# A norm's sum in four groups, a first stage in native matmuls, the next job's weights ahead of constants and gates, splits shared by two engines, an output sum moved first

## The chip, the cores and the metric

The kernel runs on one core of one Trainium2 chip, in one launch. The metric is the device time in microseconds of one execution; three runs are given, and their median stands for the kernel. A profiled execution has a time of its own, and a span (first to last recorded instruction) that is a little shorter. Engines are named as in the profile: PE (TensorE matmul), PEld (its weight load), DVE (VectorE), ACT (ScalarE), POOL (GpSimd), SP (SyncE, which here only issues DMAs).

## The reference, cut to what matters

One decoder layer with D = 2048, 256 tokens, batch 1, float32:

```python
cond = silu(c)
sh1, sc1, g1, sh2, sc2, g2 = split(cond @ mod_w + mod_b, 6)     # 6 vectors of 2048
h = rms_norm(x, norm1_g) * (1 + sc1) + sh1
a, gt = split(h @ w_in + b_in, 2)                               # 2048 x 4096
u = depthwise_causal_conv(a * sigmoid(gt), dw_w) + dw_b         # 31 taps
y = silu(layer_norm(u, ln_g, ln_b)) @ w_out + b_out             # 2048 x 2048
x = x + (1 + g1) * y
h = rms_norm(x, norm2_g) * (1 + sc2) + sh2
x = x + (1 + g2) * (square(relu(h @ mlp_w1)) @ mlp_w2)          # 2048 x 8192 x 2048
```

The six modulation vectors cost a 2048 x 12288 matrix for one row, so they are mostly traffic: 100 MB of the 301 MB that are read.

## The kernel before, in words

The text below gives the names and lines of the kernel before. Activations are kept transposed, channels on the 128 partitions in 16 tiles (`KT`), the 256 tokens along the free axis. `k` counts channel tiles, `k2` pairs of them.

**Precision.** A float32 product is made in one of two ways. *Native*: one float32 matmul with 256 columns, which the profile records as two passes (32 records for 16 matmuls). *Split*: weight and activation are each split into a rounded `hi` (ScalarE copy to fp32r) and a remainder `lo` (`lo = w - hi`, on VectorE or GpSimd), and three fast fp32r products are summed. `split_w` (L191) splits a 1 MB weight tile in two halves of 8 channel tiles: hi at L200, lo at L202. `split_act` (L208) does it for an activation pair: hi at L209, lo at L210, into a tile `hl`.

**Loads.** All large loads are 1 MB, issued by SP in one fixed list, `order` (L460 to L472). `take` (L182) hands out the next one and `top_up` issues further loads as buffers come free: `RAW` = 5 raw tiles (one more may be issued and wait on SP's queue) and `FIRST` = 4 tiles of the first stage. SP works in order, so a load that waits for its buffer holds all behind it.

**Modulation.** Two ways again. `mod_col` (L353) takes one column tile `mod_c` and multiplies and sums it against `cond` on VectorE (L358, 2.3 us). `mod_chunk` (L291) takes a row tile `mod_r` and does it with small matmuls on TensorE (L300); these lie between the jobs as filler.

**First stage** (L490 to L594, the first 141 us). Squares of x on ScalarE, their sum over the channels by matmuls with a matrix of ones into one PSUM tile (`column_sum`, L376), then `rms_factor` (L394) and `inverse_root` (L382) give r1. After that come sixteen steps of k. A step takes two modulation columns (scale and shift of channel tile k, `take_col`, VectorE in the order of `in_order`), forms h (ScalarE, L585), and adds the product of h with one 1 MB tile `first` (16 blocks of 128 x 128) into eight PSUM accumulators `held[0..7]` (the outputs of the "in" jobs 0 to 7, value and gate). Steps whose k is in `NATIVE` are native (L548). The six others split the tile: hi on ScalarE (L525), lo on VectorE (L532), three products (L552 to L554). The last tile is loaded in two halves (L176). Behind the list of the first stage stand the rest of the constants (`dwq`, 256 columns, and the second part of `vec`, 1008 columns), and then the weights of job 8.

**Jobs.** `jobs` (L437) is the list of all that follows: ("in", 8..15), ("out", 0..7), and four quarters of ("up", ...) and ("down", ...). A job has two weight tiles c = 0, 1. The loop at L769 splits the next job's weights ahead of the job's matmuls. Of the "in" jobs the outputs go through `gate` (L744: Sigmoid on ScalarE, product on VectorE into a padded tile `u`), and then through the 31-tap convolution, for eight channel tiles on VectorE (L623) and for the others on TensorE, by way of ScalarE copies into a `wide` tile (`copy_wide`, L699 to L708) and a GpSimd-made diagonal. L758 to L767 are the seam of the two stages: weights of job 8 split, the eight gates of the held outputs, the second weight tile of job 8 split between gates 1 and 2.

**Layer norm and out jobs.** L838 to L888 make the layer norm: per pair a subtraction on GpSimd (L879), a product on VectorE (L880), two Silu on ScalarE (L884), and the split by `split_act`. The out jobs follow; of each the sum is scaled and biased on ScalarE (L905), added to x on VectorE (L907), squared, scaled for the MLP, and split again (L919 to L922). ("out", 1, 0) is split early, on GpSimd.

**What sets the order.** A tile scheduler with a timeline simulation fixes each engine's order at build time, from the order of the program, priorities and its own costs. `urgent()` (L124) raises the priority of what it encloses; `tc.issue_after(ins)` demands that an instruction comes behind another. An engine then works strictly in that order and waits on semaphores. Tiles are buffers of pools; a new use waits until all uses of the old tile are through. The `conv` pool of the second stage (L597: `wide`, `diag` and others) lies where the `start` pool (L88: x and the `first` tiles) was.

Of the kernel before, what the change touches and what calls it, by code (L numbers as in the profile page):

```python
# [11 lines left out]
ALU = mybir.AluOpType  # L12
# [24 lines left out]
NATIVE = (1, 3, 5, 6, 8, 9, 11, 12, 14, 15)  # L37
# [20 lines left out]
SIDE = 14  # L58
POOLED = [("out", 0), ("out", 1), ("up", 0, 1), ("up", 0, 2)]
# [4 lines left out]
def conv_block(ctx: ExitStack, tc: tile.TileContext, x, vec, dwq, c_row, mod_r, mod_c, w_first, w_in, w_out, w1, w2, out):  # L64
# [12 lines left out]
    soon = VEC["b_in"]  # L77
# [36 lines left out]
    nc.scalar.activation(cz[:, :, 3], col("c", 0, KT), AF.Silu)  # L114
    modc = const.tile([P, 6 * KT], F32, name="modc")
# [3 lines left out]
    warm = const.tile([P, 1], F32, name="warm")  # L119

    def table(func, after):
        nc.scalar.activation(warm, after, func)
# [3 lines left out]

    raw = {}
# [3 lines left out]
    state = {"used": 0}  # L131
# [27 lines left out]
    def top_up():  # L159
        while todo and waiting[home(todo[0])] < room[home(todo[0])]:  # L160
# [13 lines left out]
            with tc.issue_after(state["load"].ins) if "load" in state else ExitStack():  # L174
                if key == ("first", KT - 1):
                    nc.sync.dma_start(raw[key][:, 0:HELD], source(key)[:, 0:HELD])  # L176
                    with tc.issue_after(state["load"].ins):
                        state["load"] = nc.sync.dma_start(raw[key][:, HELD:], source(key)[:, HELD:])
                else:
                    state["load"] = nc.sync.dma_start(raw[key], source(key))  # L180
# [8 lines left out]
    HALF = KT // 2  # L189

    def split_w(key, engine):  # L191
# [4 lines left out]
        for h in range(2):  # L196
# [3 lines left out]
            nc.scalar.activation(hi, w[:, ks, :], AF.Copy)  # L200
            with tc.issue_after(state["e_end"]) if key[0] == "out" and engine is nc.vector else ExitStack():
                end = engine.tensor_tensor(lo, w[:, ks, :], hi.bitcast(F32), op=ALU.subtract)  # L202
            if engine is nc.gpsimd:
                state["pool"] = end.ins
# [3 lines left out]
    def split_act(dst, src):  # L208
        state["hi_end"] = nc.scalar.activation(dst[:, :, 0:T], src, AF.Copy).ins  # L209
# [130 lines left out]
    def mod_finish():  # L340
        while pending:
# [3 lines left out]
            with urgent():  # L345
# [4 lines left out]
                for b, at in enumerate(ats):  # L350
                    mod_bias(at, nj, p[:, 0 : nj * n].rearrange("p (j n) -> p n j", n=n)[:, b, :])
# [30 lines left out]
    def inverse_root(ms, src, scale, r, then=None):  # L382
# [4 lines left out]
        state["root_end"] = nc.scalar.activation(guess, guess, AF.Copy, scale=-0.5).ins  # L387
        if then is not None:
            table(then, guess[:, 0:1])
        nc.vector.scalar_tensor_tensor(ms, ms, EPS, q, op0=ALU.add, op1=ALU.mult)  # L390
        nc.vector.scalar_tensor_tensor(r, ms, 3.0, guess, op0=ALU.subtract, op1=ALU.mult)
        return r

    def rms_factor(total, ms, r):  # L394
        nc.vector.tensor_scalar(ms, total, 1.0 / D, None, op0=ALU.mult)
        return inverse_root(ms, total, 1.0 / D, r)
# [65 lines left out]
    order += [("vec", 0)]  # L462
    order += [jobs[HELD] + (c,) for c in range(2)]
# [27 lines left out]
    mods(by_col(0))  # L491
# [555 lines left out]
```

## Time and profile before

| | |
|---|---|
| three runs | 1114.11, 1112.88, 1110.83 us (median 1112.88) |
| profiled execution | 1112.13 us |
| its span | 1110.3 us |
| mean granted TensorE clock | 0.994 |
| first stage | ends at 140.9 us |
| "in" jobs 8 to 15 with the convolution | to about 300 us |
| layer norm and out jobs | to about 400 us |
| MLP, four quarters | to the end |
| read from memory | 301 MB |

How to read it: times are microseconds of the span of the profiled execution. The page gives the busy time of each engine and the chain of work that ended last. Other views of the trace are used in the prediction: TensorE's waits by what released them (total, count, longest); a view of the DMA traffic in 40 slices; the chain itself, row by row (start, length, what); the timeline of a stretch (start, length of the row, engine, line, operation, output and inputs, shape, count, and in brackets the wait ahead of it and its releaser); the table of stretches (for each engine busy time and count, then granted clock, DMA share and GB/s).

### The profile page before, as it was taken

Reading aid. Unit: us, or ns where it says so; the run is one execution under the profiler, and the core shown is the slowest. Engines: PE = TensorE matmul, PEld = TensorE weight load, DVE = VectorE, ACT = ScalarE, POOL = GpSimd, SP = SyncE. Lnnn points to the kernel's source line nnn. Section 1 sums busy time; section 2 is a strip of 40 time slices with the busy share of each in tenths; the row PEclk is TensorE's granted clock in tenths of the full one; section 3 lists DMA queues with packets and bytes.
Section 4 is the critical chain, followed back from the end, with each engine's and each line's share of the span. In section 5 each row is a group of like instructions: output and inputs, shape, how many; then the busy total and the mean of one; then the engine's idle time right before and its main releaser. Section 6 shows DMA issues by size and latency. Waiting matters only on the chain.

```text
span 1110.3 us, 15575 instructions
## 1 busy us (share of the span) xinstructions
PE 1087.4 (98%) x6112; PEld 900.7 (81%) x6112; DVE 766.0 (69%) x1018; ACT 522.5 (47%) x693; POOL 161.2 (15%) x103
## 2 busy tenths in 40 slices
PE   6999899999989999999999999999999999999998
PEld 4988776666689998888888888888888888888887
DVE  4988689988379977676785567644656565565553
ACT  5222295664575578444444444333444334444441
POOL 0000087467532334000000000000000000000000
PEclk8999999999999999999999999999999999999999
DMA  9999978889499977898996879757888867788641
GB/s 386 420 420 421 417 304 349 347 319 353 170 357 369 388 260 254 260 277 269 385 394 215 236 235 296 298 157 261 249 237 236 246 206 227 224 237 249 211 143 38
DMA packets 142027, 314.24 MB, mean 283 GB/s; under 512 B 87553, under 2 KB 105473, under 8 KB 106753
## 3 DMA queue, kind: packets, MB, share of 16 engines
q1 hardware_dynamic: 141808, 313.16, 81.0%
q8 instruction: 48, 0.79, 0.3%
q14 instruction: 25, 0.20, 0.0%
q10 hardware_dynamic: 146, 0.08, 0.0%
HBM read 301.15 MB, written 12.07 MB: 282 GB/s over the span
## 4 chain that ended last, share of the span: by engine, by line
PE 87%; DMA 6%; DVE 5%; issue 1%; ACT 0%; DVEq 0%
PE mm L248 20%; PE mm L247 20%; PE mm L249 20%; PE mm L224 6%; DMA raw<-mod_c 4%; DVE raw L358 3%; PE mm L225 3%; PE mm L221 3%; PE mm L220 3%; PE mm L222 3%; PE row L300 2%; PE mm L731 2%; DMA first<-w_first 2%; DVE lo L532 1%; PE mm L548 1%
## 5 line engine op out<-in xcount | busy, mean ns | idle before, releaser
L200 ACT ACTIVATE hi<-raw 128x1024 fp32r<-128x1024 f32 x320 | 336.0, 1058 | 373.6 <-PE mm L249 322.7
L202 DVE TENSOR_TENSOR lo<-raw,hi 128x1024 fp32r<-128x1024 f32 x272 | 333.5, 1234 | 175.1 <-ACT hi L200 171.7
L248 PE MATMUL mm<-lo,u 128*128 128x512 f32 x496 | 193.0, 389 | 0.0
L247 PE MATMUL mm<-hi,u 128*128 128x512 f32 x496 | 193.0, 389 | 0.0
L249 PE MATMUL mm<-hi,u 128*128 128x512 f32 x496 | 192.9, 389 | 0.0
L249 PE MATMUL mm<-hi,hl 128*128 128x512 f32 x480 | 186.7, 389 | 0.0
L248 PE MATMUL mm<-lo,hl 128*128 128x512 f32 x480 | 186.7, 389 | 0.0
L247 PE MATMUL mm<-hi,hl 128*128 128x512 f32 x480 | 186.7, 389 | 0.0
L358 DVE SCALAR_TENSOR_TENSOR raw<-raw,cond 128x2048 f32<-128x2048 f32 x64 | 147.6, 2310 | 32.4 <-DMA raw<-mod_c 28.6
L202 POOL TENSOR_TENSOR lo<-raw,hi 128x1024 fp32r<-128x1024 f32 x48 | 114.5, 2410 | 199.8 <-ACT hi L200 199.8
L249 PEld LDWEIGHTS mm<-hi,u 128*128 128x128 f32 x496 | 93.1, 188 | 19.4
L248 PEld LDWEIGHTS mm<-lo,u 128*128 128x128 f32 x496 | 93.1, 188 | 19.1
L247 PEld LDWEIGHTS mm<-hi,u 128*128 128x128 f32 x496 | 93.1, 188 | 19.0
L247 PEld LDWEIGHTS mm<-hi,hl 128*128 128x128 f32 x480 | 90.1, 188 | 18.8
L249 PEld LDWEIGHTS mm<-hi,hl 128*128 128x128 f32 x480 | 90.1, 188 | 18.7
L248 PEld LDWEIGHTS mm<-lo,hl 128*128 128x128 f32 x480 | 90.1, 188 | 18.7
L623 DVE SCALAR_TENSOR_TENSOR acc<-u,v,acc 128x256 f32<-128x256 f32 x224 | 94.7, 489 | 1.9
L220 PE MATMUL mm<-hl,hi 128*128 128x256 f32 x288 | 81.1, 286 | 3.0 <-DVE x L907 2.6
L221 PE MATMUL mm<-hl,hi 128*128 128x256 f32 x288 | 82.0, 286 | 0.2 <-DVE hl L210 0.2
L222 PE MATMUL mm<-hl,lo 128*128 128x256 f32 x288 | 81.7, 285 | 0.0
L224 PE MATMUL mm<-hl,hi 128*128 128x512 f32 x224 | 81.5, 404 | 0.0
L225 PE MATMUL mm<-hl,lo 128*128 128x256 f32 x224 | 63.5, 284 | 0.0
(184 smaller groups left out, 1269.5 us busy)
## 6 DMA issues: line engine op xcount, KB each, us to landing
raw<-w SPq DMA_DIRECT2D x128, 1024.0 KB, 5.3
raw<-mod_c SPq DMA_DIRECT2D x64, 1024.0 KB, 11.2
raw<-mod_r SPq DMA_DIRECT2D x32, 1024.0 KB, 7.6
raw<-w_in SPq DMA_DIRECT2D x16, 1024.0 KB, 7.1
raw<-w_out SPq DMA_DIRECT2D x16, 1024.0 KB, 7.6
first<-w_first SPq DMA_DIRECT2D x15, 1024.0 KB, 16.5
flat<-two SPq DMA_DIRECT2D x30, 256.0 KB, 2.7
two<-flat SPq DMA_DIRECT2D x120, 64.0 KB, 4.3
```

Source lines behind the costliest of these rows:

```text
L200: nc.scalar.activation(hi, w[:, ks, :], AF.Copy)
L202: end = engine.tensor_tensor(lo, w[:, ks, :], hi.bitcast(F32), op=ALU.subtract)
L220: nc.tensor.matmul(out_p, w, m[:, 0:T], start=begin, stop=False)
L221: nc.tensor.matmul(out_p, w, m[:, T : 2 * T], start=False, stop=False)
L222: state["mm_end"] = nc.tensor.matmul(out_p, lo[:, k % HALF, :], m[:, 0:T], start=False, stop=end)
L224: nc.tensor.matmul(p[:, c, :], hi[:, k % HALF, :], m, start=(k == 0), stop=(k == KT - 1))
L225: state["mm_end"] = nc.tensor.matmul(p[:, c, T : 2 * T], lo[:, k % HALF, :], m[:, 0:T], start=False, stop=(k == KT - 1), skip_group_check= ...
L247: nc.tensor.matmul(p, p_hi, hi, start=begin, stop=False)
L248: nc.tensor.matmul(p, p_hi, lo, start=False, stop=False)
L249: nc.tensor.matmul(p, p_lo, hi, start=False, stop=end)
L358: nc.vector.scalar_tensor_tensor(w, w, 1.0, cb, op0=ALU.mult, op1=ALU.mult, accum_out=acc)
L623: nc.vector.scalar_tensor_tensor(out, s, w, acc, op0=ALU.mult, op1=ALU.add)
```

## The change

**First stage.** The set `NATIVE` and all splits of the first stage go: every step is native (`first_mm` takes the raw tile). The squares of x are made by ScalarE for pairs 0 to 3 and by VectorE for pairs 4 to 7. Their sum goes with 32 columns of ones into four groups of 32 partitions, is copied once by ScalarE, and is folded by one further matmul, which gives 32 times the sum; `inverse_root` takes that scale into its constants, and a VectorE pass goes in both RMS norms. The ScalarE table for the root is asked for ahead, and the columns of step 0 come behind the squares in the program. The last two columns and the last weight tile (`SPLIT_LOADS`) are loaded in halves, and the products of those two columns are made by halves (`mod_col_halves`).

**Constants.** `soon` now reaches to the taps: b_in, dwb, lng, lnb and b_out come with the first vector load (96 columns more). The rest is loaded behind the first weight tile of job 8, not ahead of it.

**The seam.** The first weight tile of job 8 is split with high priority, its first half's lo on VectorE, the second on GpSimd. Gates 0 to 7 all have high priority; the second weight tile is asked for behind gate 5, with `issue_after` between gates and splits.

**Layer norm and out jobs.** `split_act` makes hi on ScalarE for even pairs and on VectorE for odd ones. The hi of ("out", 1, 1) comes after the last Silu. The modulation biases of `mod_finish` come after the last split (`lo_end`). The scaling on ScalarE and the addition to x of each out job become urgent.

The diff, cut:

```diff
-NATIVE = (1, 3, 5, 6, 8, 9, 11, 12, 14, 15)
+SPLIT_LOADS = [("col", SC1 * KT + KT - 1), ("col", SH1 * KT + KT - 1), ("first", KT - 1)]
-    soon = VEC["b_in"]
+    soon = VEC["dww"]
+    table(AF.Abs_reciprocal_sqrt, cond[:, KT - 1, 0:1])
...
-                if key == ("first", KT - 1):
...
+                if key in SPLIT_LOADS:
+                    first_half = nc.sync.dma_start(raw[key][:, 0:HALF], source(key)[:, 0:HALF])
+                    with tc.issue_after(first_half.ins):
+                        state["load"] = nc.sync.dma_start(raw[key][:, HALF:], source(key)[:, HALF:])
...
-            nc.scalar.activation(hi, w[:, ks, :], AF.Copy)
+            with tc.issue_after(state["silu"]) if key == ("out", 1, 1) else ExitStack():
+                state["w_hi"] = nc.scalar.activation(hi, w[:, ks, :], AF.Copy).ins
+            by = nc.vector if key == ("in", HELD, 0) and h == 0 else engine
...
-                end = engine.tensor_tensor(lo, w[:, ks, :], hi.bitcast(F32), op=ALU.subtract)
+                end = by.tensor_tensor(lo, w[:, ks, :], hi.bitcast(F32), op=ALU.subtract)
...
-    def split_act(dst, src):
-        state["hi_end"] = nc.scalar.activation(dst[:, :, 0:T], src, AF.Copy).ins
+    def split_act(dst, src, on_act=True):
+        if on_act:
+            state["hi_end"] = nc.scalar.activation(dst[:, :, 0:T], src, AF.Copy).ins
+        else:
+            nc.vector.tensor_copy(dst[:, :, 0:T], src)
...
-                    mod_bias(at, nj, ...)
+                    with tc.issue_after(state["lo_end"]) if "lo_end" in state else ExitStack():
+                        mod_bias(at, nj, ...)
...
+    def mod_col_halves(at):
+        w = take(("col", at))
+        which, k = divmod(at, KT)
+        accs = [modc[:, at : at + 1], other]
+        for h in range(2):
+            ks = slice(h * HALF, (h + 1) * HALF)
+            in_order(lambda: nc.vector.scalar_tensor_tensor(
+                w[:, ks, :], w[:, ks, :], 1.0, cond[:, ks, :], op0=ALU.mult, op1=ALU.mult, accum_out=accs[h]
+            ))
+        in_order(lambda: nc.vector.scalar_tensor_tensor(
+            accs[0], accs[0], other, col("modb", at), op0=ALU.add, op1=ALU.add
+        ))
...
-    def rms_factor(total, ms, r):
-        nc.vector.tensor_scalar(ms, total, 1.0 / D, None, op0=ALU.mult)
-        return inverse_root(ms, total, 1.0 / D, r)
+    def rms_factor(total, ms, r, times=1):
+        return inverse_root(ms, total, 1.0 / (times * D), r)
...
-    order += [("vec", 0)]
-    order += [jobs[HELD] + (c,) for c in range(2)]
+    order += [jobs[HELD] + (0,), ("vec", 0), jobs[HELD] + (1,)]
...
-        nc.scalar.activation(s, pair_of(xs, k2), AF.Square)
-        column_sum(p[:, 0:T], [s[:, j, :] for j in range(2)], k2 == 0, k2 == HALF - 1)
+        if k2 < HALF // 2:
+            nc.scalar.activation(s, pair_of(xs, k2), AF.Square)
+        else:
+            nc.vector.tensor_tensor(s, pair_of(xs, k2), pair_of(xs, k2), op=ALU.mult)
+        for j in range(2):
+            g = (2 * k2 + j) % 4
+            nc.tensor.matmul(p[32 * g : 32 * g + 32, 0:T], ones[:, 0:32], s[:, j, :], start=k2 < 2, stop=k2 >= HALF - 2)
+    mods(by_col(0))
+    with urgent():
+        part = two()[:, 0, :]
+        nc.scalar.activation(part, p[:, 0:T], AF.Copy)
+        p = ps.tile([P, 512], F32, name="row", bufs=1)
+        nc.tensor.matmul(p[:, 0:T], ones, part, start=True, stop=True)
+        r1 = tmp.tile([P, T], F32, name="r", bufs=1)
+        rms_factor(p[:, 0:T], p[:, T : 2 * T], r1, 32)
...
-    split_w(jobs[HELD] + (0,), nc.gpsimd)
     with urgent():
-        for i in range(2):
+        split_w(jobs[HELD] + (0,), nc.gpsimd)
+        take(("vec", 0))
+        with tc.issue_after(state["w_hi"]):
+            gate(0, held[0])
+        for i in range(1, 6):
             gate(i, held[i])
-    with tc.issue_after(state["sg"].ins):
-        split_w(jobs[HELD] + (1,), nc.gpsimd)
-    with urgent():
-        for i in range(2, HELD):
-            gate(i, held[i])
+        with tc.issue_after(state["sg"].ins):
+            split_w(jobs[HELD] + (1,), nc.gpsimd)
+        with tc.issue_after(state["w_hi"]):
+            gate(6, held[6])
+        gate(7, held[7])
...
-                    split_act(new_hl(k2), f)
+                    split_act(new_hl(k2), f, k2 % 2 == 0)
...
-            for c in range(2):
-                k = 2 * i + c
-                nc.scalar.activation(t2[:, c, :], t2[:, c, :], AF.Identity, scale=mcol(G1, k), bias=gb[:, k : k + 1])
             xp = pair_of(xs, i)
-            nc.vector.tensor_tensor(xp, t2, xp, op=ALU.add)
+            with urgent():
+                for c in range(2):
+                    k = 2 * i + c
+                    nc.scalar.activation(t2[:, c, :], t2[:, c, :], AF.Identity, scale=mcol(G1, k), bias=gb[:, k : k + 1])
+                nc.vector.tensor_tensor(xp, t2, xp, op=ALU.add)
```

In the changed kernel the native matmuls are line 550, the hi and lo of `split_w` lines 203 and 206, the output addition line 905, the `wide` copies line 700, the gates line 738.

83 lines of the change are left out of this document (24 added, 59 removed).

## The prediction

> **What bounds the kernel now.** I read the page first, then the chain that ended last, then TensorE's waits, the DMA view of the first 160 us, and the timeline at three places. From the page:
>
> ```profile
> span 1110.3 us, 15575 instructions
> PE 1087.4 (98%) x6112; PEld 900.7 (81%) x6112; DVE 766.0 (69%) x1018; ACT 522.5 (47%) x693; POOL 161.2 (15%) x103
> PE 87%; DMA 6%; DVE 5%; issue 1%; ACT 0%; DVEq 0%
> ```
>
> TensorE is the bound, and the 11% of the chain that is DMA and DVE must lie where TensorE waits for them. TensorE's waits from 141 us to the end:
>
> ```profile
> PE mm L220 <- DVE x L907: 2.6, 1, 2.6
> PE row L300 <- DMA raw<-mod_r: 0.8, 1, 0.8
> PE mm L220 <- ACT hl L209: 0.4, 1, 0.4
> PE mm L221 <- DVE hl L210: 0.2, 1, 0.2
> ```
>
> So after 141 us only 4.0 us are waited, 2.6 of them at one place (line 907). An edit behind 141 us pays there or nowhere, and a wait that it adds there is paid in full. Before 141 us the DMA view (40 slices of 4 us) and the chain say:
>
> ```profile
> GB/s 162 420 428 424 424 416 422 424 422 414 424 420 420 418 416 422 424 424 424 420 414 424 416 424 422 422 418 418 424 420 416 406 419 422 416 221 223 268 141 420
> 116.91 2.31 DVE raw L358 x2
> 121.53 2.22 DVE raw L358 x2
> 123.94 1.15 DVE lo L532
> 127.30 3.45 PE mm L548 x16
> 134.21 3.45 PE mm L548 x16
> ```
>
> The queue moves 420 GB/s without a pause to 140 us. The sixteen steps of the first stage need 3.15 MB each (two modulation columns and a weight tile), so a step can't be served faster than every 7.5 us. At its end TensorE runs behind the loads: step 13 waits for the last DVE split (line 532), so steps 14 and 15 stand back to back after it.
>
> **The change part by part.**
>
> *First stage, all steps native, last loads halved.* A native step starts at 127.14 and the next at 134.04: 6.90 us, under the 7.5 us of its loads. The six split steps lose 12 DVE and 12 ACT passes; DVE then has about 5.8 us of work a step. The rows of the end:
>
> ```profile
> 107.58 4.39 SPq L180 DMA_DIRECT2D raw<-mod_c  x2
> raw<-mod_c SPq DMA_DIRECT2D x1, 1024.0 KB, 15.1
> 127.14 3.61 PE L548 MATMUL mm<-two,first 128*128 128x256 f32 x16
> 127.79 2.28 DVE L358 SCALAR_TENSOR_TENSOR raw<-raw,cond 128x2048 f32<-128x2048 f32 x1
> 130.12 0.16 DVE L338 TENSOR_TENSOR modc<-modc,v 128x1 f32<-128x1 f32 x1
> 130.31 0.60 ACT L585 ACTIVATE two<-two,modc,amp 128x256 f32<-128x256 f32 x1 [5.23 <-DVE modc L338]
> 134.04 3.62 PE L548 MATMUL mm<-two,first 128*128 128x256 f32 x16
> ```
>
> The last column load is issued at 107.58 + 4.39 - 0.33 = 111.6 and lands 15.1 later, at 126.7; the one of step 14 lands a pitch earlier, at 119.2. In the change nothing ahead of them in the queue is larger except 48 KB of the vector, so I keep both. Step 14: 119.2 + 2.3 (product) + 0.2 + 0.7 (line 585) and some 0.2 of semaphores = 122.6, ending at 129.5. Step 15: the halves of its last column are done at 128.7 (the first from 126.3 to 127.5 behind the column before it, the second 1.2 more), + 0.2 + 0.7 = 129.7, just behind step 14. So it starts at 129.7, not 134.04, and the stage ends at 129.7 + 6.9 = 136.6 instead of 140.9: **-4.3 us**.
>
> *Norm's sum in four groups, squares on two engines, rsqrt table early.* Step 0 starts at 25.31 before; with the shorter chain I work it out at about 19. Step by step, TensorE gains 0.6 us on the loads and has caught up by step 7 from either start within 2.4 us, so this is cover for the native steps, and I count nothing more for it. If it failed, the stage would end up to 2.4 us later.
>
> *Next job's weights ahead of the constants.* The first weight tile of job 8 lands about 131.9 and is split by 136.5, as DVE now takes half of it. Job 8 can follow at 136.6. This goes with the -4.3.
>
> *What this meets: the order on ACT.* In the changed program as built, ACT's order after the first split is gates 0, 1, 2, then twelve `wide` copies (line 700), then gates 3, 4, 5, and only then the hi passes of job 8's second tile. The first `wide` copy waits for TensorE's last native matmul, since its buffer lies where x and the `first` tiles were. Before, all gates and those hi passes came ahead of the copies:
>
> ```profile
> 136.34 1.99 ACT L200 ACTIVATE hi<-raw 128x1024 fp32r<-128x1024 f32 x2
> 137.47 7.08 POOL L202 TENSOR_TENSOR lo<-raw,hi 128x1024 fp32r<-128x1024 f32 x3 [135.53 <-ACT hi L200]
> 138.24 0.83 ACT L746 ACTIVATE two<-mm,v 128x256 f32<-128x256 f32 x2
> 142.63 4.49 ACT L708 ACTIVATE wide<-u 32x284 f32<-32x284 f32 x10
> 146.60 0.40 PE L224 MATMUL mm<-hl,hi 128*128 128x512 f32 x1
> 146.83 0.28 PE L225 MATMUL mm<-hl,lo 128*128 128x256 f32 x1
> ```
>
> From the end of the stage, 136.6: 0.1, twelve copies of 0.449 = 5.4, three gates of 0.415 = 1.25, one hi pass 1.05, and then POOL's lo pass of 7.08/3 = 2.4 with two hand-overs of 0.1: 10.4 us, 147.0. Behind it stand the second half of job 8 on TensorE (in order), the hi passes of job 9, gates 6 and 7, and DVE's taps. TensorE reaches that lo at 136.6 + 5.9 = 142.5 and waits 4.5 us (2.3 for hi, one matmul, 2.2 for lo). Before it used that lo at 146.83, so from here the change is at **+0.2 us**: the stage's gain is gone. Taps start at about 143.9 against 142.54, which DVE's 3.7 us of idle time at 161 us covers; I count 0. Without that cover a job boundary could cost TensorE about 1 us.
>
> *Clock after that wait.* No row shows such a pair of pauses. The nearest is the pause at line 907:
>
> ```profile
> 329.51 0.28 PE L222 MATMUL mm<-hl,lo 128*128 128x256 f32 x1
> 332.41 0.58 PE L220 MATMUL mm<-hl,hi 128*128 128x256 f32 x1 [2.62 <-DVE x L907]
> 335.32 0.28 PE L221 MATMUL mm<-hl,hi 128*128 128x256 f32 x1
> 332.00:336.00 4.00, 3.59 (x19) 3.59 (x20) 4.00 (x7) 2.22 (x6) 1.05 (x1) 0.59 0.99 377
> 26.00:32.00 6.00, 6.00 (x32) 6.00 (x32) 5.96 (x8) 1.89 (x4) 0.00 (x0) 0.54 1.01 422
> ```
>
> Here a pause of 2.8 us (329.63 to 332.41) is followed by 13 matmuls in 2.9 us that take 0.12 each elsewhere: 1.35 lost, at a mean clock of 0.59. At the start (clock 0.54 for 6 us) about 3 us are lost. So 0 to 3, and I take the nearest row: **+1.35**.
>
> *Output sum first, splits shared.* The 2.8 us pause comes from DVE's order: the sum of out job 0 stands behind products and splits, the last of which followed an ACT pass that had waited for a load:
>
> ```profile
> 329.02 2.00 ACT L200 ACTIVATE hi<-raw 128x1024 fp32r<-128x1024 f32 x2 [2.55 <-DMA raw<-w_out]
> 330.54 1.22 DVE L202 TENSOR_TENSOR lo<-raw,hi 128x1024 fp32r<-128x1024 f32 x1
> 331.67 0.68 DVE L907 TENSOR_TENSOR x<-mm,x 128x512 f32<-128x512 f32 x1
> 319.75 0.69 DVE L210 TENSOR_TENSOR hl<-acc,hl 128x512 fp32r<-128x512 f32 x1 [1.00 <-ACT hl L209]
> raw<-mod_c SPq DMA_DIRECT2D x1, 1024.0 KB, 16.6
> 304.78 14.62 SPq L180 DMA_DIRECT2D raw<-mod_c  x2
> ```
>
> In the change four of the eight hi copies go to DVE, ACT needs 16 x 0.57 + 4 x 0.6 + 0.5 = 12 us from 303.3, and DVE's last norm split ends at about 316.6, not 320.4. Ahead of the sum there then stand two products and three splits, not three and four; the second product's load lands at 304.8 + 16.6 = 321.4. That gives 321.5 + 2.3 + three splits and hi waits (to 326.3) + 0.7 = 327.0, ahead of 329.6, when TensorE wants the buffer. So the pause and its slow matmuls go: 2.8 + 1.35 = **-4.1**. Late next is nothing near: the next weights are split 5 us ahead. The norm's own waits (0.4 + 0.2) stay, as its first pair keeps its path. The four DVE copies (0.6 each) fit in the 6 us that DVE idles there. Between 320 and 398 us DVE is full in before too, starts 3.8 us earlier and does no more, so I count 0; if the loads hold it back instead, up to 4.1 is lost again (a rival).
>
> *Smaller.* One DVE pass less in each mean-square root (0.43): no wait of TensorE shows there, 0. The b_in constants moved into the first vector load: in time, 0.
>
> **Sum**: +0.2 + 1.35 - 4.1 = -2.6 us. On the profiled execution, 1112.13 us with 1.8 of it outside the span, this gives 1109.5; that execution lies 0.75 under the median, and on the median of 1112.88 it is **1110.3 us**.
>
> **The rivals.**
>
> 1. *TensorE keeps its clock over the wait in job 8.* For it: each of the two pauses is under 2.4 us, shorter than the 2.8 us that cost the clock at 329 us. Against: only one matmul stands between them. Then -2.6 - 1.35 = -3.9: 1109.0. [...]
> 2. *The other side: the output sum is still late.* Place: DVE between 317 and 327 us, in order; the second product waits for its modulation load. If that lands more than 2.6 us after 321.4, the sum passes 329.6 and the pause is back, slow matmuls and all. For it: the queue is at 344 to 426 GB/s from 304 to 320 us, and the waiting split on ACT shows that loads run late there. Price 4.1: -2.6 + 4.1 = +1.5, 1114.4, slower than before. If besides the clock stays at half for 6 us in job 8, 1116.
> 3. *The wait in job 8 is not there*, because the copies run in the shadow of the last step and the stage's gain stays: -4.3 - 4.1 = -8.4, 1104.5. Against: the wait on the last native matmul is in the program. This is the change doing what it says in full.
>
> **How the numbers follow.** Forecast 0.44; rival 1 0.24; rival 2 0.22 (0.06 of it with the long half rate); rival 3 0.10. A measurement of this kernel can tell about 0.3%, 3.3 us, from no change: faster means under 1109.5, slower over 1116.2. Faster: rival 3, two thirds of rival 1, a quarter of the forecast: 0.37. Slower: the long end of rival 2, and a tenth, out of the other cases, for waits at job boundaries that I cost at nothing (1 us each, and their clock): 0.16. Within: 0.47. The range reaches from 1 us above rival 3, 1105.5 (part of the stage's gain kept), to rival 2 with the long half rate, 1116.0.
>
> **What would show it.** Right: line 550's last step starts near 129.7 us; no group of line 206 or 203 is left in the first stage; TensorE waits about 4.5 us in the second half of job 8, for ACT and POOL (lines 203 and 206); the granted clock dips behind it; no wait of a matmul for the sum of line 905. Wrong: steps that follow each other at 6.9 us to the very end (TensorE bound, the stage ending after 137), the twelve copies before 136 us, or waits at line 231 in later jobs.

## The result, and the profile after

Five runs of each kernel on one chip: the kernel before 1112.88 us median (1110.83 to 1114.24), the changed kernel **1117.99 us** (1116.96 to 1120.38). The ratio is 1.0049 with a 95% interval of 1.0031 to 1.0068: half a per cent slower, where 1110.3 was forecast and the range ended at 1116.0. The profiled execution of the changed kernel is its slowest, 1120.38 us with a span of 1118.6, so its trace shows 8.3 us more span than that of before, 3.2 more than the medians differ by. The mean granted clock of that execution was 0.991, and 0.997 or 0.998 in the four others, so the clock losses read from the trace below are not those of a typical execution. In the experiments one execution of 1829 us (all out edits undone, the traced one) and one of 2213 us (the sums of out jobs 0 and 1 first) are slow ones that the medians leave out.

From the changed kernel's page:

```profile
span 1118.6 us, 15367 instructions
PE 1092.7 (98%) x6018; PEld 897.3 (80%) x6018; DVE 761.7 (68%) x1018; ACT 506.6 (45%) x675; POOL 164.9 (15%) x102
```

TensorE's waits from 141 us on (total, count, longest), all but two of 0.2:

```profile
PE mm L227 <- ACT hi L203: 2.2, 1, 2.2
PE mm L231 <- ACT hi L203: 2.2, 1, 2.2
PE mm L232 <- POOL lo L206: 1.9, 1, 1.9
PE mm L227 <- ACT hl L214: 1.4, 1, 1.4
PE mm L227 <- DVE x L905: 0.9, 1, 0.9
PE mm L231 <- DVE u L740: 0.6, 1, 0.6
PE mm L229 <- DVE lo L206: 0.6, 1, 0.6
```

Where there were 4.0 us of waits behind 141 us, there are now about 10. Since nearly all of TensorE's matmuls are the same in both kernels from job 8 on, the two traces can be laid on each other: the start of the same matmul, changed kernel less kernel before.

| place | start before | changed less before |
|---|---|---|
| first matmul of job 8 | 140.76 | -3.35 |
| first lo matmul of its second tile | 146.83 | +1.08 |
| job 9 | 153.44 | +4.66 |
| out job 0 | 305.09 | +4.68 |
| ahead of the pause in front of out job 2 | 323.87 | +4.88 |
| half of out job 2 | 339.52 | +1.86 |
| second tile of out job 6 | 385.60 | +1.86 |
| second tile of out job 7 | 397.12 | +7.78 |
| MLP, last matmul | 1106.41 | +8.08 |

The first stage itself, first and last step of the changed kernel:

```profile
19.33 5.82 PE L550 MATMUL mm<-two,first 128*128 128x256 f32 x16 [4.55 <-ACT two L581]
130.69 3.62 PE L550 MATMUL mm<-two,first 128*128 128x256 f32 x16
```

So there are four steps: the first stage gains 3.35, the seam loses 8.0, the pause in front of out job 2 gives back 3.0, and a place that the prediction did not have, out job 7, loses 5.9. The seam, on ScalarE and TensorE of the changed kernel (start, length, operation, in brackets the wait):

```profile
137.85 5.40 ACT L700 ACTIVATE wide<-u 32x284 f32<-32x284 f32 x12 [1.89 <-issue]
143.27 0.47 ACT L738 ACTIVATE two<-mm,v 128x256 f32<-128x256 f32 x1
143.65 0.83 ACT L738 ACTIVATE two<-acc,v 128x256 f32<-128x256 f32 x2
144.36 2.01 ACT L203 ACTIVATE hi<-raw 128x1024 fp32r<-128x1024 f32 x2
145.47 0.49 PE L231 MATMUL mm<-hl,hi 128*128 128x512 f32 x1 [2.16 <-ACT hi L203]
147.91 0.58 PE L232 MATMUL mm<-hl,lo 128*128 128x256 f32 x1 [1.94 <-POOL lo L206]
```

ScalarE starts the copies right behind TensorE's last native matmul, which ends at 137.77 (the trace names no releaser, the program makes them wait for it). It makes twelve copies and three gates, and only then the hi that TensorE wants from 143.3 on. And the stretches at half clock behind the two stalls (columns: the stretch, its length, busy time and count of PE, PEld, DVE, ACT and POOL, then the granted clock, DMA share and GB/s):

```profile
146.50:153.33 6.83, 5.42 (x16) 4.31 (x17) 6.83 (x19) 6.68 (x13) 6.83 (x4) 0.50 0.32 95
395.68:402.50 6.82, 6.27 (x28) 5.97 (x29) 4.46 (x4) 6.79 (x10) 2.10 (x2) 0.50 0.92 315
```

5.42 us of matmuls at half rate in job 8 are 2.7 us lost, 6.27 in out job 7 are 3.1.

### The profile page after: what moved, and what is told of

It reads as the page before. It is cut to its first block, busy times and chain, and to the rows that moved or that the text cites. A ratio compares the mean times of both kernels' runs of the same rounds, so it can differ in the third digit from the quotient of the medians.

```text
span 1118.6 us, 15367 instructions
## 1 busy us (share of the span) xinstructions
PE 1092.7 (98%) x6018; PEld 897.3 (80%) x6018; DVE 761.7 (68%) x1018; ACT 506.6 (45%) x675; POOL 164.9 (15%) x102
## 4 chain that ended last, share of the span: by engine, by line
PE 78%; DMA 12%; DVE 6%; ACT 2%; issue 2%; POOL 1%; ACTq 0%; SPq 0%; POOLq 0%; DVEq 0%
PE mm L255 20%; PE mm L254 20%; PE mm L256 20%; DMA raw<-mod_c 8%; PE mm L231 4%; PE mm L227 3%; PE mm L229 3%; PE mm L228 2%; DVE raw L381 2%; DMA raw<-w_in 2%; PE mm L232 2%; DVE acc L615 2%; PE row L307 1%; DMA raw<-w_out 1%; ACT wide L700 1%
## 5 line engine op out<-in xcount | busy, mean ns | idle before, releaser
L255 PEld LDWEIGHTS mm<-lo,u 128*128 128x128 f32 x496 | 93.1, 188 | 19.3 <-DVE lo L206 0.4
L227 PE MATMUL mm<-hl,hi 128*128 128x256 f32 x288 | 82.7, 289 | 4.4 <-ACT hi L203 2.2
L229 PE MATMUL mm<-hl,lo 128*128 128x256 f32 x288 | 82.8, 288 | 0.6 <-DVE lo L206 0.6
L228 PE MATMUL mm<-hl,hi 128*128 128x256 f32 x288 | 82.7, 288 | 0.2 <-DVE hl L217 0.2
L550 PE MATMUL mm<-two,first 128*128 128x256 f32 x256 | 60.7, 392 | 8.5 <-ACT two L581 8.5
```

Of the source, the lines that this page charges most:

```text
L227: nc.tensor.matmul(out_p, w, m[:, 0:T], start=begin, stop=False)
L228: nc.tensor.matmul(out_p, w, m[:, T : 2 * T], start=False, stop=False)
L229: state["mm_end"] = nc.tensor.matmul(out_p, lo[:, k % HALF, :], m[:, 0:T], start=False, stop=end)
L255: nc.tensor.matmul(p, p_hi, lo, start=False, stop=False)
L550: step = nc.tensor.matmul(held[n][:, c, :], w[:, 2 * n + c, :], h, start=k == 0 and c == 0, stop=k == KT - 1, skip_group_check=True)
```

## The experiments

My theory after the two traces: (a) ScalarE's order at the seam costs 8 us; (b) the edits of the out jobs moved the pause in front of out job 2 to out job 7, where it is longer. Rivals: the weights come too late whatever the order; VectorE is simply full in the out jobs. Medians of five rounds beside the kernel before (1112.6 to 1112.7 us in all three sets).

**The seam alone.**

```diff
         gate(7, held[7])
+    state["seam"] = state["sg"].ins
...
+                    with tc.issue_after(state["seam"]) if ct == 0 else ExitStack():
+                        nc.scalar.activation(dst, src, AF.Copy)
-                    nc.scalar.activation(dst, src, AF.Copy)
```

> The changed kernel with one edit: ScalarE's sixteen wide copies of channel tile 0 come behind gate 7, so the splits of job 8's second weight tile and all gates stand ahead of them. Theory (ScalarE's order at the seam cost the stage's gain): the two waits of TensorE in job 8 (2.2 for hi, 1.9 for lo) and the half-rate stretch behind them go; the lo that TensorE wanted at 143.1 and got at 147.9 is there in time. 4.8 + 2.7 = 7.5 less than 1118.0: 1110.5 us, and job 9 starts near 150.5 on the span instead of 158.1. Rival (the weights of job 8 land or are split too late whatever the order, since GpSimd needs 2.4 us for each half): a wait of 2 us or more stays in job 8, and the time is 1114 to 1117. The later stages may be ordered anew by the scheduler, which can add or take some 3 us in the out jobs.

Measured: 1113.3 us, ratio 1.0006 (0.9997 to 1.0015). ScalarE's order and its effect:

```profile
137.46 2.02 ACT L203 ACTIVATE hi<-raw 128x1024 fp32r<-128x1024 f32 x2
140.07 4.49 ACT L701 ACTIVATE wide<-u 32x284 f32<-32x284 f32 x10
```

No wait is left in job 8, and job 9 starts 4.66 us ahead of the kernel before instead of 4.66 behind; at 273 us this kernel leads by 3.37. (1.2 of the 4.66 ahead is a filler that stands later.) The seam is (a), shown: 8.1 us between the two traces. But 3.37 ahead at 273 us became 1.1 behind in out job 7: the out jobs lose 4.4 us here too. In the medians the edit brings 4.7 us, and the total missed its 1110.5 by 2.8.

**ScalarE's order in front of out job 7.** The stall of the changed kernel is here:

```profile
391.29 1.22 DVE L217 TENSOR_TENSOR u<-two,u 128x512 fp32r<-128x512 f32 x1
392.43 2.28 DVE L381 SCALAR_TENSOR_TENSOR raw<-raw,cond 128x2048 f32<-128x2048 f32 x1
393.42 1.11 ACT L904 ACTIVATE mm<-mm,gb,modc 128x256 f32<-128x256 f32 x2 [4.81 <-PE mm L229]
394.46 1.99 ACT L203 ACTIVATE hi<-raw 128x1024 fp32r<-128x1024 f32 x2
395.55 0.49 PE L227 MATMUL mm<-hl,hi 128*128 128x256 f32 x1 [2.17 <-ACT hi L203]
```

ScalarE stands 4.8 us idle in front of a scaling that waits for TensorE's last matmul of out job 6, with the hi that TensorE wants next right behind it.

```diff
-            with urgent():
+            with urgent(), tc.issue_after(state["w_hi"]) if i in (6,) else ExitStack():
                 for c in range(2):
```

> The changed kernel with one edit: ScalarE's scaling of out job 6 comes behind the hi splits of job 7's weights (nothing else changes place but the four lo splits and one product behind them on VectorE). Theory (the stall in front of out job 7 is ScalarE's order: the hi stood behind a scaling that itself waited for TensorE's last matmul of job 6): the waits of 2.2 and 0.55 us at 393 to 397 and the half-rate stretch behind them (some 3.3 us) go: 1118.0 - 5.9 = 1112.1. Rival (job 7's weights land too late, as their loads are issued 5 us later than before): the wait stays, between 1116 and 1118.

Measured: 1119.19 us, ratio 1.0056 (1.0044 to 1.0069): no gain. The hi now come at 390.05, ahead of the scaling. TensorE waits all the same, 2.3 us for a lo:

```profile
390.05 2.01 ACT L203 ACTIVATE hi<-raw 128x1024 fp32r<-128x1024 f32 x2 [1.38 <-DMA raw<-w_out]
392.50 2.28 DVE L381 SCALAR_TENSOR_TENSOR raw<-raw,cond 128x2048 f32<-128x2048 f32 x1
394.71 4.62 DVE L206 TENSOR_TENSOR lo<-raw,hi 128x1024 fp32r<-128x1024 f32 x4
```

My theory of ScalarE's order falls. VectorE is busy without a break from 383.5 to 394.71 and has the lo behind that; the weights landed only at 390.0 (wait on the load). VectorE is late, and so are the raw buffers that it frees and the loads that wait for them. The loads of out job 7's weights, first in the kernel before, then in the changed one:

```profile
375.45 3.15 SPq L180 DMA_DIRECT2D raw<-w_out  x2
382.83 3.34 SPq L184 DMA_DIRECT2D raw<-w_out  x2
```

They are issued 7.4 us later, where TensorE is only 1.9 us later. All four come right behind the end of a lo pass of VectorE.

**The wait for the last Silu undone.**

```diff
-            with tc.issue_after(state["silu"]) if key == ("out", 1, 1) else ExitStack():
-                state["w_hi"] = nc.scalar.activation(hi, w[:, ks, :], AF.Copy).ins
+            state["w_hi"] = nc.scalar.activation(hi, w[:, ks, :], AF.Copy).ins
```

> The changed kernel with one edit undone: the hi split of the second weight tile of out job 1 no longer waits for the layer norm's last Silu. Theory (this edit put GpSimd's two lo passes beside VectorE's busy stretch and held the raw buffers): GpSimd's lo passes come back to an earlier time, VectorE's first product after the norm takes 2.3 us instead of 4.25 and the next lo 1.2 instead of 3.35; the second product's load is issued some 5 us earlier; the built order has the hi of job 7 ahead of the scaling of job 6, so the stall of 5.9 us goes: near 1112, the wait of 0.9 for the sum may come or go. Rival (the edit is harmless, and VectorE's long product has another reason): 4.25 us stays, 1116 to 1118.

Measured: 1117.38 us, ratio 1.0043 (1.0029 to 1.0057). The first fence is the changed kernel's, the second this one's:

```profile
321.85 2.40 POOL L206 TENSOR_TENSOR lo<-raw,hi 128x1024 fp32r<-128x1024 f32 x1 [7.22 <-ACT hi L203]
322.16 4.25 DVE L381 SCALAR_TENSOR_TENSOR raw<-raw,cond 128x2048 f32<-128x2048 f32 x1
324.20 4.46 POOL L206 TENSOR_TENSOR lo<-raw,hi 128x1024 fp32r<-128x1024 f32 x1
326.40 3.35 DVE L206 TENSOR_TENSOR lo<-raw,hi 128x1024 fp32r<-128x1024 f32 x1
308.44 18.32 SPq L184 DMA_DIRECT2D raw<-mod_c  x2
```

```profile
320.53 4.76 POOL L206 TENSOR_TENSOR lo<-raw,hi 128x1024 fp32r<-128x1024 f32 x2 [6.12 <-ACT hi L203]
326.30 2.28 DVE L381 SCALAR_TENSOR_TENSOR raw<-raw,cond 128x2048 f32<-128x2048 f32 x1
330.79 1.21 DVE L206 TENSOR_TENSOR lo<-raw,hi 128x1024 fp32r<-128x1024 f32 x1
308.23 17.42 SPq L184 DMA_DIRECT2D raw<-mod_c  x2
```

The mechanism of the stretched passes is as expected. With GpSimd's two passes 1.3 us earlier and VectorE idle beside most of them, GpSimd needs 4.76 instead of 6.82, VectorE's product 2.28 instead of 4.25, the lo behind the products 1.21 instead of 3.35; the stall in front of out job 7 is gone. One expectation missed: the second product's load is issued at 308.23 against 308.44, not 5 us earlier, and the one behind it in the same row 1.1 us earlier. The total is not as expected either: three products stand ahead of the sum again, as in the kernel before, where the changed kernel has two, and TensorE waits 2.7 us for the sum in front of out job 2. At the end of the trace this kernel is 5.05 behind the one before, 4.47 of it already at 305 us, from the seam. The edit trades one stall for another.

**All edits of the layer norm and the out jobs undone**, the first stage and the seam as changed. (The `urgent()` around scaling and sum is one of them; with that one alone undone the built order is the same on every engine, so it moves nothing.)

```diff
-                    split_act(new_hl(k2), f, k2 % 2 == 0)
+                    split_act(new_hl(k2), f)
...
-            with tc.issue_after(state["silu"]) if key == ("out", 1, 1) else ExitStack():
-                    with tc.issue_after(state["lo_end"]) if "lo_end" in state else ExitStack():
-            with urgent():                  # around the out job's scaling and sum
```

> The changed kernel with all edits of the layer norm and the out jobs undone (splits by ScalarE alone, no wait for the last Silu, biases not held back, scaling and sum not urgent); first stage and seam stay as changed. Theory (out edits: -3.0 at the pause in front of out job 2, +5.9 in front of out job 7): the pause of 2.8 us and its half-rate stretch come back, the stall goes: 1118.0 - 2.9 = 1115.1, that is +2 on the kernel before, and all of it lies between 137 and 160 us. Rival (the first stage and the seam cost more than the 4.7 us that I read at 305 us): 1117 or more.

Measured: 1116.43 us, ratio 1.0034 (1.0022 to 1.0046), between the two expectations and nearer to the second. No trace of it can be laid beside the others. It is 1 us under the run before, with overlapping intervals: what is left of the out edits without the Silu wait brings no gain.

**Both places mended.**

```diff
+    state["seam"] = state["sg"].ins         # and the wide copies behind it, as in the first run
...
-            with tc.issue_after(state["silu"]) if key == ("out", 1, 1) else ExitStack():
```

> The changed kernel with two edits: the wide copies behind gate 7, and the hi split of out job 1's second weights no longer behind the last Silu. Theory (the two places are separate and add up): job 8 follows the first stage without a wait, so the kernel is 3.4 us ahead of the one before at 305 us; the pause of about 2.7 us in front of out job 2 is there as in the kernel before, no stall in front of out job 7. 1112.6 - 3.4 = 1109.2 us. Rival (what is gained at the seam is lost again by VectorE in the out jobs, as in the run with the seam edit alone): 1112 to 1113.

Measured: 1109.82 us, ratio 0.9971 (0.9959 to 0.9982). As the theory had it: 3.1 us ahead at 305 us, the pause in front of out job 2 as before (2.2 us), 3.09 ahead at the end. That the two places add up is not so in the medians: apart the edits bring 4.7 and 0.6 us, together 8.2. Apart, each leaves a loss in the out jobs: the seam alone a stall in front of out job 7, the other one the pause in front of out job 2.

**The sum put first by hand**, since `urgent()` didn't do it: products and lo splits that are asked for later come behind the sum of out job 0.

```diff
-                nc.vector.tensor_tensor(xp, t2, xp, op=ALU.add)
+                end = nc.vector.tensor_tensor(xp, t2, xp, op=ALU.add)
+            if i == 0:
+                state["e_end"] = end.ins
```

> The kernel of the run before in this list with one edit more: on VectorE the sum of out job 0 comes ahead of all column products and lo splits that are asked for behind it. Theory (the pause in front of out job 2 is VectorE's order): TensorE's wait for that sum and the half-rate stretch behind it go, 3 to 4 us less in front of out job 3. Theory, second part (VectorE is the bound of the out jobs: what it puts off there it owes later): TensorE waits for a lo or hi split, or for a sum, in the out jobs that follow, and most of it is given back: 1108 to 1110 us. Rival (VectorE has room): 1105.5 to 1106.5, no new wait.

Measured: 1113.21 us, ratio 1.0002 (0.9993 to 1.0011), 3.4 slower than without. TensorE's waits of this kernel from 300 to 410 us:

```profile
PE mm L229 <- DVE lo L206: 6.2, 4, 2.3
PE mm L227 <- ACT hl L214: 1.4, 1, 1.4
```

The pause is gone: this kernel leads the one before by 7.46 us at 340 us. Then four waits for lo splits of 6.2 us in all take it back, and it ends 0.3 ahead. What VectorE paid for the early sum stands in its own row:

```profile
323.17 0.69 DVE L907 TENSOR_TENSOR x<-mm,x 128x512 f32<-128x512 f32 x1 [5.04 <-ACT mm L906]
```

It stood idle for 5.04 us in front of the sum, until ScalarE's scaling was through, with products and lo splits held behind it. That it comes out worse than the pause I did not expect; the second part of the theory holds in sign, its size was too small. What an early sum would bring without this wait of VectorE the run does not show.

**The sums of out jobs 0 and 1 first.**

```diff
-            if i == 0:
+            if i < 2:
                 state["e_end"] = end.ins
```

> As the run before, and the sum of out job 1 put first too. By the theory that VectorE is the bound, the same total within 1.5 us, with the wait at another job; by the rival that only the order counts, the faster of the two: 1105 to 1106.

Measured: 1113.24 us, ratio 1.0002 (0.9993 to 1.0011), with again 6.2 us in four waits for a lo, and again 5.04 us of VectorE idle in front of the first sum. Same total, other order: that fits VectorE's time as the bound of the out jobs.

**TensorE's clock by itself.**

```diff
+    def pause(lengths):
+        for length in lengths:
...
+                first = nc.tensor.matmul(p[:, 0:128], ones, ones, start=True, stop=True)
...
+                nc.scalar.activation(d, p[:, 0:128], AF.Copy)
+                for _ in range(length - 1):
+                    nc.scalar.activation(d, d, AF.Copy)
...
+                    state["tok_end"] = nc.tensor.matmul(p[:, 128:256], ones, d, start=True, stop=True).ins
```

> The kernel before with ten pauses of TensorE put into the MLP, 43 us apart: a small matmul, then 1, 2, 3, 4, 6 or 8 dependent ScalarE copies, then a small matmul that reads the last; at the end twice a pair of pauses (2 and 2, 3 and 3 copies) with one matmul between. It measures the clock loss by itself. By the one row that I had (2.8 us idle, then 3.4 us at half rate) pauses of about 2 us and less cost only themselves, those of 3 us and more cost 1.4 to 1.7 us besides. By the two stretches of the changed kernel (4.1 us in two parts, and 2.2 us, each followed by 6.8 us at half rate) pauses of 2 us already cost up to 3.4 us besides, and the length of the half-rate stretch is a multiple of 3.4 us. [...]

Measured: one execution, 1147.32 us. Two of the ten pauses, and the clock behind each; a matmul's bracket is its wait:

```profile
637.95 0.49 PE L784 MATMUL row<-gap,ones 128*128 128x128 f32 x2 [1.84 <-ACT gap L782]
783.77 0.49 PE L784 MATMUL row<-gap,ones 128*128 128x128 f32 x2 [3.49 <-ACT gap L782]
```

```profile
638.57:641.99 3.42, 3.42 (x10) 2.65 (x9) 0.00 (x0) 0.00 (x0) 0.00 (x0) 0.50 0.98 283
782.40:785.80 3.40, 2.03 (x10) 1.74 (x11) 0.12 (x1) 1.23 (x4) 0.00 (x0) 1.00 0.93 347
785.80:789.20 3.40, 3.40 (x17) 2.81 (x16) 1.07 (x1) 1.06 (x1) 0.00 (x0) 1.00 0.96 393
```

A pause of 1.84 us cost 3.42 us at half clock, and one of 3.49 us cost nothing besides itself. Neither expectation has that. What the trace shows instead: the half-rate stretches begin at 590.79, 638.57, 686.36 and 734.15, always a whole number of 3.413 us apart (14 each). So in this trace they lie on a grid of 3.41 us windows, and how much of one such window was idle told more than the length of the pause. Worked out from the waits above and their rows' starts:

| pause, us | idle in its idlest window | half rate after |
|---|---|---|
| 2.06 | 1.50 | none |
| 2.41 | 2.41 | 3.41 |
| 1.84 | 1.84 | 3.42 |
| 2.18 | 2.18 | 3.41 |
| 2.81 | 2.28 | 3.41 |
| 3.49 | 1.84 | none |
| 1.49 + 0.77 | 1.49 | none |
| 1.83 + 1.11 | 1.83 | none |

With 2.18 us idle of 3.41 or more the clock went to half for a window, in which TensorE loses 1.7 us (3.41 us at a granted clock of 0.50); with 1.50 or less it did not. At 1.84 it went to half once and once not, so the idle time alone does not decide there.

**GpSimd for VectorE, out jobs 3 and 5**, on top of the sum put first.

```diff
-POOLED = [("out", 0), ("out", 1), ("up", 0, 1), ("up", 0, 2)]
+POOLED = [("out", 0), ("out", 1), ("out", 3), ("out", 5), ("up", 0, 1), ("up", 0, 2)]
```

> The kernel with the sum of out job 0 put first (1113.2 us, four waits of 6.2 us in all for lo splits), and the eight lo splits of out jobs 3 and 5 made by GpSimd instead of VectorE. Theory A (VectorE is short of time and GpSimd has it): 8 x 1.2 = 9.8 us less on VectorE, more than the 6.2 that TensorE waited: 1106 to 1107 us. Theory B (a GpSimd pass beside a busy VectorE stretches both, as in the changed kernel, where two passes cost VectorE 4.2 us): 8 passes free 9.8 us and cost up to 17: no gain, 1112 to 1118, with VectorE's products at 3 to 4 us beside GpSimd's passes.

Measured: 1122.72 us, ratio 1.0093 (1.0078 to 1.0108), slower even than theory B's end. VectorE's and GpSimd's groups from 305 to 400 us, first the kernel before, then this one (busy, mean ns of one):

```profile
L358 DVE SCALAR_TENSOR_TENSOR raw<-raw,cond 128x2048 f32<-128x2048 f32 x15 | 35.6, 2384 | 0.0
L202 POOL TENSOR_TENSOR lo<-raw,hi 128x1024 fp32r<-128x1024 f32 x2 | 4.8, 2411 | 4.3 <-ACT hi L200 4.3
```

```profile
L381 DVE SCALAR_TENSOR_TENSOR raw<-raw,cond 128x2048 f32<-128x2048 f32 x14 | 42.9, 3084 | 0.0
L206 POOL TENSOR_TENSOR lo<-raw,hi 128x1024 fp32r<-128x1024 f32 x10 | 35.1, 3537 | 13.1 <-ACT hi L203 13.1
```

One of the products of this kernel, and four lo passes of GpSimd around it, in the timeline:

```profile
365.15 15.98 POOL L206 TENSOR_TENSOR lo<-raw,hi 128x1024 fp32r<-128x1024 f32 x4
374.40 4.49 DVE L381 SCALAR_TENSOR_TENSOR raw<-raw,cond 128x2048 f32<-128x2048 f32 x1
```

Products take up to 4.49 us and GpSimd's lo 3.5 on average instead of 2.4; TensorE waits for lo of GpSimd (3.2 in all), for a sum (3.3) and for hi (2.2).

**GpSimd for VectorE, out job 2**, on top of the sum put first.

```diff
-POOLED = [("out", 0), ("out", 1), ("up", 0, 1), ("up", 0, 2)]
+POOLED = [("out", 0), ("out", 1), ("out", 2), ("up", 0, 1), ("up", 0, 2)]
```

> The kernel with the sum of out job 0 put first, and the four lo splits of out job 2 made by GpSimd. Theory A (VectorE short of time): 4 x 1.2 = 4.9 us less on VectorE ahead of all later sums, TensorE's 6.2 us of waits for lo fall to 1.3 or less: 1107 to 1109. Theory B (GpSimd's passes stretch VectorE's, and need 2.4 us and more each, 10 us for the job): the waits stay or move to out job 2 itself: 1112 to 1116.

Measured: 1115.78 us, ratio 1.0031 (1.0020 to 1.0043): theory B again, 2.6 slower than with VectorE alone.

**Native steps alone, in the kernel before.**

```diff
-NATIVE = (1, 3, 5, 6, 8, 9, 11, 12, 14, 15)
+NATIVE = tuple(range(16))
```

> The kernel before with one edit: all sixteen steps of the first stage native, nothing else. Theory (the last VectorE split held step 13, and native steps keep pace with the loads): step 15 starts near 131, the last column being made in one piece (some 1 us later than in halves), the stage ends near 138.5 instead of 140.9, and job 8 follows at once, as the old order of ScalarE has its splits ahead of the copies: -2.4 us, 1110.3. Rival (the gain needs the shorter norm, the early weights or the halved loads): within 1 us of 1112.7.

Measured: **1109.03 us**, ratio 0.9966 (0.9955 to 0.9978).

```profile
123.94 3.72 PE L548 MATMUL mm<-two,first 128*128 128x256 f32 x16 [0.95 <-ACT two L585]
130.95 3.62 PE L548 MATMUL mm<-two,first 128*128 128x256 f32 x16
137.67 0.58 PE L224 MATMUL mm<-hl,hi 128*128 128x512 f32 x1
138.52 0.38 PE L225 MATMUL mm<-hl,lo 128*128 128x256 f32 x1 [0.27 <-POOL lo L202]
```

Job 8 starts at 137.67 us; in the changed kernel, with the short norm, the halved loads and the early weights, it starts at 137.41. One line has all but 0.26 us of the first stage's gain, and the seam needs no mending here.

**Seam mended, all out edits undone.** The edits of the first and the fourth run together:

```diff
+                    with tc.issue_after(state["seam"]) if ct == 0 else ExitStack():
...
-                    split_act(new_hl(k2), f, k2 % 2 == 0)
+                    split_act(new_hl(k2), f)
```

> The changed kernel with the wide copies behind gate 7 and all edits of the layer norm and the out jobs undone. If the shared splits, the biases held back and the urgent sum bring nothing, it is the 1109.8 us of the kernel that had only the wait for the last Silu undone, within 0.7. If they bring what I had counted (the pause in front of out job 2 gone), this one is 3 to 4 us slower, 1113; if they cost, it is faster, 1108.

Measured: 1108.71 us, ratio 0.9969 (0.9958 to 0.9980). The shared splits, the biases held back and the urgent sum bring nothing: the kernel that has them had a ratio of 0.9971, and this one waits 2.6 us for the sum as the kernel before does. These two and the one-line kernel are the fastest and can't be told apart: some 3 to 4 us under the kernel before, 8 to 9 under the changed one.

## Why the prediction was wrong, point by point

Two terms of the sum failed: the out jobs, taken at -4.1 with nothing lost behind, and the clock behind the wait at the seam, taken at +1.35.

- *First stage, all steps native.* Right in mechanism, 0.9 short in size: step 0 at 19.3 (about 19), step 15 at 130.7 (129.7), the end, counted as there, at 137.6 where 136.6 was worked out, so -3.35 and not -4.3. The halves of the last loads, the shorter norm and the early weights are worth 0.26 us together, as the native steps alone showed.
- *The order on ScalarE at the seam.* Right: copies, three gates, hi, GpSimd's lo, in that order, with lo at 147.9 where 147.0 was worked out; the 0.9 is the later end of the stage.
- *Clock after that wait.* Here the size failed: 1.35 was taken, 2.7 measured in the trace, because the half rate lasted two windows (6.83 us) and not one. The lo 1.1 later than before, 2.7 of clock and a wait of 0.6 for a gate are 4.4 of the +4.7 at 305 us, where +1.55 was forecast. Rival 1, no clock loss, was wrong in this trace. In the four other executions a granted clock of 0.997 leaves room for some two half-rate windows in all (an estimate: 0.003 of 1116 us is 3.3 us, two windows of 3.41 us at half rate), where the traced one has six, two of them at the start; so there the rival may have held. They are only 2.2 to 3.4 us shorter, less than the 5.8 us of clock that the trace lost behind its two stalls, and how the rest comes about is not shown. In the prediction I had compared the pauses by their length, under 2.4 us against 2.8; in the run with the pauses 3.49 us cost nothing besides itself and 1.84 us a window at half rate, so the length is the wrong quantity.
- *Output sum first, splits shared.* This step failed, "So the pause and its slow matmuls go: 2.8 + 1.35 = -4.1" and "starts 3.8 us earlier and does no more, so I count 0". The trace has -3.0 at out job 2 and +5.9 at out job 7. I had the sum at 327.0, and it started at 334.8. The second product's load, which I had taken as the last of what it waits for, did not hold it: issued at 308.4, it took 17.5 us to land, and the product ran only at 330.2. VectorE itself did: its first product took 4.25 us and the lo behind it 3.35, beside GpSimd's late lo passes. From there on the buffers come free late: the next modulation load was issued 7.4 us later than before (at 326.4, right behind that product), and so were out job 7's weights. This is the loss that I put at nothing; with the wait for the last Silu undone, the stall in front of out job 7 was gone. That TensorE waited only 0.9 us for the sum is due to its own 4.9 us of delay from the seam, and so the -3.0 is in part luck: with the seam alone mended it waited 1.8 us there, and a window at half rate followed (329.53 to 332.95). VectorE was full in the kernel before (77.9 of 78 us from 320 to 398), but that an earlier out job 2 must be paid for later is not shown: with the sum put first by hand 4.1 us were won at the pause and 7.2 lost behind it, yet VectorE had idled 5.0 us for it. My rival 2 had the right sign; the load it named was not the cause, and the loss came at out job 7.
- *The wait for the last Silu* I had noted as a part of the diff and never priced. It moved GpSimd's passes beside VectorE's busy stretch, 4.1 us of VectorE (4.25 and 3.35 against 2.28 and 1.21). In the trace of before the row was there to be seen: a product of 2.75 instead of 2.28 (from 339.24 us) beside one of GpSimd's `sqacc` additions.
- *Smaller edits at nothing*: no wait of TensorE in the trace speaks against it. The urgent sum, which belongs to the step above, moved no instruction at all.

The profile after shows the sum of it: +1.55 - 4.1 = -2.6 was forecast, +4.7 - 3.0 + 5.9, and 0.3 in the MLP, were measured in the trace. In the medians it is +5.1, with fewer half-rate windows by the granted clock.

## What to carry to other kernels

A pause of a bound engine that ends on a full engine may be that engine's debt: moving the one instruction forward only moved the pause here, and made the full engine wait as well. Whether less work on the full engine takes the pause away is not shown: the runs that took lo splits from it gave them to GpSimd, and were slower. When an order is planned by a scheduler, the edit that gains (here one line) is best tried alone, because each further edit re-orders what lies behind it. And an operation moved to another time must be looked at beside its new neighbours, on another engine too: here VectorE's product took 4.25 us beside GpSimd's lo passes and 2.28 without them.

## What the runs showed of the hardware

- In these traces TensorE's half rate lies on a grid of 3.413 us: in one execution all half-rate stretches begin at the same phase of it (146.50 and 395.68 in the changed kernel are 73 windows apart). Over thirteen traces of this case, from 45 us on, a window at full rate with 1.88 to 2.80 us without a matmul was always followed by half rate, one with 1.50 or less never. Between, both occur: 1.62 (in both runs with more splits on GpSimd), 1.76, 1.77 (the seam alone) and 1.84 were followed by it, 1.65 twice, 1.83 and 1.84 were not. What else decides stays open. In these runs pauses of 1.8 to 3.5 us cost nothing, 1.7 or some 3 us more, and their length did not tell which (3.49 us cost nothing, 1.84 us 1.7). The same wait of 2.6 us for the out sum cost a half-rate window in the kernel before (331.85 to 335.27) and none in the kernel with native steps, which passed it 1.26 us cheaper. That this is behind the differences between executions of one kernel is not shown: with the seam alone, executions at a granted clock of 0.992 took 1112.9 to 1114.9 us and those at 0.997 took 1113.0 to 1113.3.
- Half rate lasted one window or two. In job 8 the stall went on into the next window (146.50 to 149.92, with 1.41 idle). Why it was two after 2.2 us in front of out job 7 (0.55 idle in the next window) and one after 2.8 us in the kernel before (0.56 idle in the next) stays open.
- VectorE's products and lo splits and GpSimd's lo passes took longer where they overlapped: a product 4.25 us (4.49 with more splits on GpSimd) instead of 2.28, GpSimd's second lo pass 4.46 instead of 2.40, VectorE's lo 3.35 instead of 1.21. In the changed kernel's rows above, GpSimd's first pass took its 2.40 us, and each of the three instructions behind it lasted until the other engine's had ended, and then about as long as it takes alone: the product ran 2.15 us beyond the end of GpSimd's first pass (324.25), GpSimd's second pass 2.26 beyond the end of the product (326.40), VectorE's lo 1.09 beyond the end of that pass (328.66). So in these rows the one that came second got through only behind the other, which fits that splits moved to GpSimd brought nothing (1122.72 and 1115.78 us against 1113.21).
